# A decoder layer's prompt scores: from 64-row fp32 products to stacked full-height rounded ones

## The chip, the cores and the metric

The kernel runs on one core of a Trainium2 chip. The metric is the device time of one launch in microseconds. Before the change three runs took 1153.15, 1154.85 and 1155.16 us; the median is 1154.85. A core has five engines with a queue each: TensorE (PE, with its weight loads shown as PEld), VectorE (DVE), ScalarE (ACT), GpSimd (POOL) and SyncE (SP), which here issues the loads.

## The reference

One layer of a hybrid decoder, for a prompt of 512 tokens with 16 meta tokens ahead of it and for 8 samples of 8 new tokens, each with 2048 cached ones. The width is 1024.

```python
h = rmsnorm(x) @ w_in                     # q, k, v; GDN's q, k, v, z, b, a; two gates
# differential attention: 4 heads, two maps (m) of 64 columns each
s = einsum('bqhmd,bkhmd->bhmqk', q_blk * 64 ** -0.5, k)
s = where(k_pos <= q_pos, s, -inf)
pr = softmax(s)
o_a = einsum('bhqk,bkhe->bqhe', pr[:, :, 0] - lam * pr[:, :, 1], v)
# gated DeltaNet (GDN): causal convolution of width 4, then 4 heads in chunks of 64 tokens
mix = sigmoid(gate_a) * (o_a @ w_branch_a) + sigmoid(gate_b) * (o_b @ w_branch_b)
x = x + rmsnorm(mix @ w_out)
# ConvFFN of width 2816: up-projected gate rows, causal convolution of width 3, GELU
up, gate = split(rmsnorm(x) @ w_ffn_in)
x = x + rmsnorm((gelu(dwconv(gate)) * up) @ w_down)
```

Everything is float32, with an accuracy near that of float32 throughout.

## The kernel before

**Precision.** A float32 matrix is split into a rounded part `hi`, cast to float32r, and a rest `lo`, the difference. A product is then three rounded products: hi x hi, lo x hi and hi x lo. `split` does this for weights: ScalarE casts and VectorE subtracts (`whi`, `wlo`, lines 314 and 315). Products of plain float32 exist too; one of these leaves two records in the trace. All products are issued by the helper `mm` (line 272), all transposes at line 420, so a product is known by its tiles: `ps_d` and others with `xhi`, `xlo` are projections of the normed input, `ps_s` with `KT`, `qb` or `page`, `pT` the sampled attention over the paged cache (32 columns of the array wide), `ps_m` the prompt scores.

**Prompt attention.** For each of the four heads `da_keys` makes the keys and the values: a projection to `kvt` (128 rows: 64 of map 0 over 64 of map 1; columns are tokens), from which GpSimd copies `kT` for the scores. The scaled queries `qT` of all heads were made before, in the same layout. `prompt_rows` then takes four blocks of 128 queries. Block i has n = 16 + 128(i+1) keys: 144, 272, 400, 528. A score product multiplies 64 rows of `qT` by 64 rows of `kT`, map 0 on rows 0 to 63 and map 1 on rows 64 to 127 of the array; the two maps' results stand side by side in the one tile `ps_m`, which has one buffer. [...] VectorE's `score` moves a result to `S0` or `S1`, adds the causal mask to the last 128 keys and keeps the row maximum in `mx`; ScalarE takes the exponential, VectorE combines the maps, TensorE transposes and multiplies by the values.

**FFN.** The input projection of the FFN has 22 steps, each for 128 columns of gate and 128 of up. The activations stand as four quadrants: two halves of the 1024 rows and two halves of the tokens of 290 columns each. The first PLAIN steps multiply plainly: 8 half-depth products of 12 matmuls, 96 matmuls in all. The other steps use a scheme of seven products (`p1` to `p7`, tiles `ps_t`, `ps_g`, `ps_d`, `ps_s`) over sums of weight blocks (`sw`, split to `hw`, `lw`) and sums of activation blocks (made once, from `gf` to `fhit`, `flot`): 7 x 12 = 84 matmuls.

**What sets the order.** Each part is a Python generator. `merge` interleaves them: it advances the one whose share of work is furthest behind, counting work only on TensorE, and a `yield DELAY[k]` keeps a stream out until that many microseconds of modelled TensorE work have been issued. There are 31 delays, from the GDN chain (0 to 20), the key making (21), the prompt attention (22 to 25) and the sampled attention (26 to 30). A scheduler then fixes the order on each engine, and on the chip each engine runs its list in order, with waits on semaphores. Tiles come from pools with a fixed number of buffers; a tile's first write waits until the last reader of the buffer's former tile is done. The pool `gproj` holds, among others, `pre` (two buffers, the GDN convolution's input, from `conv_tile`), `kt` and `vt` (its results).

Of the kernel before, what the change touches and what calls it, by code (L numbers as in the profile page):

```python
# [18 lines left out]
SEQ = 512  # L19
NM = 16  # L20
# [15 lines left out]
NT = SEQ + NS + NM  # L36
CS = SEQ
CM = SEQ + NS
# [14 lines left out]
def _lay_out_constants():  # L53
# [76 lines left out]


DELAY = (
    13.61, 3.59, 0.94, 0.6, 6.0, 1.52, 1.66, 1.43, 1.32, 1.05, 0.93, 0.17, 26.0, 0.69, 0.9, 0.77,
    0.09, 0.85, 0.38, 2.28, 0.14, 0.6, 0.74, 2.36, 6.91, 0.77, 1.4, 5.18, 1.38, 1.46, 12.26,
)
KEYS = 2
CUT_S = 832
# [2 lines left out]
WRAW, WLO = 3, 4  # L140
LOADS_AHEAD = 5
NC = 290
PLAIN = 3
TAILS = 4
FINE = 8
MAIN_1 = 600.0
# [4 lines left out]
class Body:  # L151
# [1008 lines left out]
    def da_keys(self, pool, h, res):  # L1160
        nc, a, o = self.nc, self.a, self.o
        w = a["w_in"][0]
        for part, c0 in ((0, C_K), (1, C_V)):
            wt = self.weight(w, c0 + 128 * h)
            full = self.t(pool, [128, NT], "kvt", bufs=2)
            for half in HALF_T:
                out = []
                yield from self.dense_steps(wt, self.x, half, out)
                for p, c in out:
                    nc.scalar.copy(full[:, c[0] : c[1]], p)  # L1170
                yield DELAY[21] if half is HALF_T[1] else 0.0
            if part == 0:
                kT = self.t(pool, [128, NM + SEQ], "kT", bufs=KEYS)
                nc.gpsimd.tensor_copy(kT[:, NM:], full[:, 0:SEQ])
                nc.gpsimd.tensor_copy(kT[:, 0:NM], full[:, CM:NT])
                nc.gpsimd.tensor_copy(self.kTm[:, h], full[:, CM:NT])
                nc.gpsimd.tensor_copy(self.kTs[:, h, :], full[:, CS:CM])
            p1 = self.ps4("t")
            for i in range(4):
                self.transpose(p1[:, i], full[:, 128 * i : 128 * i + 128])  # L1180
            p2 = self.ps("t")
            self.transpose(p2[:NTL, :128], full[:, CS:NT])
            nat = self.t(pool, [128, 4, 128], "kno" if part == 0 else "v", bufs=2 if part == 0 else KEYS)
            if part == 0:
                tail = self.t(pool, [128, 128], "knt", bufs=2)
                op = o["new_k_prompt"][0, 0, :, h].rearrange("t m d -> t (m d)")
                os = o["new_k_sample"][0, :, :, h].rearrange("b t m d -> (b t) (m d)")
            else:
                tail = self.vt[:, 128 * h : 128 * h + 128]
                op = o["new_v_prompt"][0, 0, :, h]  # L1190
                os = o["new_v_sample"][0, :, :, h].rearrange("b t e -> (b t) e")
            nc.vector.tensor_copy(nat, p1)
            nc.vector.tensor_copy(tail[:NTL], p2[:NTL, :128])
            nc.gpsimd.dma_start(op[NM:].rearrange("(i p) e -> p i e", p=128), nat)
            nc.gpsimd.dma_start(os, tail[0:64])
            nc.gpsimd.dma_start(op[14:16], tail[64:66])
            nc.gpsimd.dma_start(op[0:14], tail[66:80])
            yield 0.0
        res.update(kT=kT, v=nat)

    def lam(self, tmp):
        nc, a, keep = self.nc, self.a, self.keep
# [77 lines left out]
    def prompt_rows(self, pool, h, st, on, order):  # L1280
        nc = self.nc
        kT, v = st["kT"], st["v"]
        e = slice(128 * h, 128 * h + 128)
        for i in order:
            n = NM + 128 * (i + 1)
            pr = [self.t(pool, [128, 528], f"S{m}", bufs=2) for m in range(2)]
            mxs = [self.t(self.keep, [128, 2], "mx", bufs=4) for m in range(2)]
            cuts = ((0, n),) if n <= 512 else ((0, n - 128), (n - 128, n))
            for lo, hi in cuts:
                p = self.t(self.psum_m, [128, 2, 512], "ps_m", bufs=1)[:, :, : hi - lo]  # L1290
                for m in range(2):
                    r = slice(64 * m, 64 * m + 64)
                    self.mm(p[:, m], self.qT[r, h, 128 * i : 128 * i + 128], kT[r, lo:hi], start=True, stop=True)
                for m in range(2):
                    s, mx = pr[m], mxs[m]
                    w = n - 128 - lo
                    if lo < n - 128:
                        self.score(s[:, lo : n - 128], p[:, m, :w], self.zeros(w), -3e38, mx[:, 0:1])
                    if hi == n:
                        self.score(s[:, n - 128 : n], p[:, m, w:], self.c("causal"), mx[:, 0:1], mx[:, 1:2])  # L1300
            rs = []
            for s, mx in zip(pr, mxs):
                nm = self.t(self.keep, [128, 1], "nm", bufs=4)
                nc.vector.tensor_scalar(nm, mx[:, 1:2], -1.0, None, op0=ALU.mult)
                sm = self.t(self.keep, [128, 1], "sm", bufs=4)
                nc.scalar.activation(s[:, :n], s[:, :n], AF.Exp, bias=nm, accum_out=sm)
                rc = self.t(self.keep, [128, 1], "rc", bufs=4)
                nc.vector.reciprocal(rc, sm)
                if s is pr[1]:
                    nc.vector.tensor_tensor(out=rc, in0=rc, in1=self.nlam, op=ALU.mult)  # L1310
                rs.append(rc)
            yield DELAY[24]
            nc.vector.tensor_scalar(pr[1][:, :n], pr[1][:, :n], rs[1], None, op0=ALU.mult)
            at = pr[0]
            nc.vector.scalar_tensor_tensor(
                out=at[:, :n], in0=at[:, :n], scalar=rs[0], in1=pr[1][:, :n], op0=ALU.mult, op1=ALU.add
            )
            aT = self.t(pool, [128, 5, 128], "aT", bufs=2)
            tp = self.ps4("t")
            for j in range(i + 1):  # L1320
                self.transpose(tp[:, j], at[:, NM + 128 * j : NM + 128 * j + 128])
            nc.scalar.copy(aT[:, : i + 1], tp[:, : i + 1])
            tq = self.ps("t")
            self.transpose(tq[:NM, :128], at[:, 0:NM])
# [445 lines left out]
    def ffn_in(self, firsts, sf, gx):  # L1770
# [203 lines left out]

        sts, waiting = [{"m": m} for m in range(PLAIN)], []
        st = sts[0]
# [23 lines left out]
        for st in sts[2:]:  # L2000
# [5 lines left out]
            plain_end(st)  # L2006
        nxt = loads(PLAIN)
        weights_g(nxt)
# [200 lines left out]
```

## Time and profile before

| what | value |
| --- | --- |
| runs | 1153.15, 1154.85, 1155.16 us |
| the profiled execution's own time | 1153.75 us |
| its span, first to last instruction | 1152.0 us |
| mean granted TensorE clock | 0.996 |
| instructions | 23616 |
| memory read / written | 146.12 / 9.88 MB |

The profiled execution is a single run; its span leaves out 1.75 us around the first and the last instruction. Busy times count the records of an engine and don't say that it ran at its best. A row of a view names the source line, the engine, the operation, output and input tiles without their numbers, shape and type. What stands in brackets or behind the bar is the engine's idle time just before, and what ended it. A float32r product is shown with type f32.

### The profile page before, as it was taken

To read this page: it belongs to the slowest core of one execution; us is meant where nothing else is said; L and a number is where in the kernel's file an instruction comes from. 1 tells how busy PE (TensorE), PEld (TensorE's weight loads), DVE (VectorE), ACT (ScalarE), POOL (GpSimd) and SP (SyncE) were. 2 spreads that over 40 slices of the span, in tenths; PEclk is the share of its full clock that TensorE was granted. 3 is DMA by queue.
4 is the path that set the end of the run, shared out by engine and by line. 5 is a ranking of instruction groups with operands and counts; after the bars stand their busy time and mean duration, and the time that the engine had idled before them with its cause. 6 is when DMAs were issued, how large, how long until landed. Compare 5 with 4: busy or idle time off the path is not lost.

```text
span 1152.0 us, 23616 instructions
## 1 busy us (share of the span) xinstructions
PE 1115.3 (97%) x8683; PEld 1004.1 (87%) x8683; DVE 717.3 (62%) x1875; ACT 539.0 (47%) x1308; POOL 220.5 (19%) x342
## 2 busy tenths in 40 slices
PE   6999999999999999999999999999999999999997
PEld 5887887787787787789999977899999999999996
DVE  5456666695486377474343765499889889832323
ACT  5334445464464365352332344365565656732321
POOL 2022221020120010010000003333455444200000
PEclk9999999999999999999999999999999999999999
DMA  7366335737756956823232364323333332432322
GB/s 208 81 223 188 102 104 195 255 110 251 237 159 216 290 173 209 263 74 80 55 90 69 110 187 153 95 70 102 102 87 100 93 94 73 144 97 74 102 75 83
DMA packets 184347, 157.56 MB, mean 137 GB/s; under 512 B 12570, under 2 KB 146273, under 8 KB 184231
## 3 DMA queue, kind: packets, MB, share of 16 engines
q1 hardware_dynamic: 179713, 147.53, 42.0%
q0 software_dynamic: 3264, 5.16, 1.5%
q10 hardware_dynamic: 1254, 3.35, 1.0%
q8 instruction: 69, 1.13, 0.4%
q14 instruction: 47, 0.39, 0.1%
HBM read 146.12 MB, written 9.88 MB: 135 GB/s over the span
## 4 chain that ended last, share of the span: by engine, by line
PE 73%; issue 13%; DVE 6%; ACT 3%; POOL 3%; DMA 1%; SPq 0%; DVEq 0%; POOLq 0%; ACTq 0%
PE ps_d L272 26%; PE ps_t L272 18%; PE ps_g L272 15%; PE ps_s L272 7%; PE ps_t L420 7%; ACT KT L1399 1%; PE ps_m L272 1%; DVE cy L650 1%; DMA lk<-in_da_lambda_k 1%; POOL grr L384 1%; POOL gf L384 0%; DVE wlo L315 0%; DMA page<-in_cache_v 0%; POOL hss L384 0%; DVE row L970 0%
## 5 line engine op out<-in xcount | busy, mean ns | idle before, releaser
L272 PE MATMUL ps_d<-xhi,whi 128*128 128x256 f32 (+2 forms) x704 | 217.8, 310 | 0.2 <-DVE qm L1128 0.2
L315 DVE TENSOR_TENSOR wlo<-wraw,whi 128x512 fp32r<-128x512 f32 x196 | 137.9, 720 | 122.4 <-ACT whi L314 121.6
L272 PE MATMUL ps_d<-xhi,wlo 128*128 128x256 f32 (+2 forms) x704 | 213.3, 303 | 0.7 <-DVE wlo L315 0.7
L272 PE MATMUL ps_d<-xlo,whi 128*128 128x256 f32 (+2 forms) x704 | 212.8, 303 | 0.3 <-DVE xlo L315 0.2
L314 ACT CAST whi<-wraw 128x512 fp32r<-128x512 f32 (+1 forms) x198 | 117.3, 612 | 179.1 <-PE ps_d L272 93.8
L272 PEld LDWEIGHTS ps_d<-xhi,whi 128*128 128x128 f32 x704 | 133.6, 190 | 5.8 <-issue 4.2
L272 PEld LDWEIGHTS ps_d<-xlo,whi 128*128 128x128 f32 x704 | 133.9, 190 | 3.3 <-issue 2.4
L272 PEld LDWEIGHTS ps_d<-xhi,wlo 128*128 128x128 f32 x704 | 133.6, 190 | 2.5 <-issue 1.0
L1399 ACT COPY KT<-ps_t 128x512 f32<-128x512 f32 x106 | 57.2, 603 | 31.3 <-PE ps_t L420 30.8
L420 PE MATMUL ps_t<-consts,page 128*128 128x128 f32 x512 | 67.8, 279 | 0.3
L272 PE MATMUL ps_t<-fhit,hw 128*128 128x290 f32 x228 | 68.0, 298 | 0.0
L272 PE MATMUL ps_t<-flot,hw 128*128 128x290 f32 x228 | 67.7, 297 | 0.0
L272 PE MATMUL ps_t<-fhit,lw 128*128 128x290 f32 x228 | 67.6, 297 | 0.0
L420 PEld LDWEIGHTS ps_t<-consts,page 128*128 128x128 f32 x512 | 55.6, 140 | 13.8 <-issue 6.7
L314 ACT CAST hw<-sw 128x512 fp32r<-128x512 f32 x76 | 47.2, 622 | 41.4 <-PE ps_g L272 19.9
L315 DVE TENSOR_TENSOR lw<-sw,hw 128x512 fp32r<-128x512 f32 x76 | 60.1, 790 | 6.7 <-ACT hw L314 6.6
L272 PEld LDWEIGHTS ps_t<-flot,hw 128*128 128x128 f32 x228 | 43.2, 190 | 0.0
L272 PEld LDWEIGHTS ps_t<-fhit,lw 128*128 128x128 f32 x228 | 43.1, 189 | 0.0
L272 PEld LDWEIGHTS ps_t<-fhit,hw 128*128 128x128 f32 x228 | 43.0, 189 | 0.0
L1887 DVE SCALAR_TENSOR_TENSOR fy<-fpre,fw,fy 128x592 f32<-128x592 f32 x44 | 36.5, 830 | 2.5 <-ACT fy L1885 1.8
L272 PE MATMUL ps_s<-page,pT 128*32 128x256 f32 x512 | 35.3, 385 | 1.8 <-DMA page<-in_cache_v 1.6
L272 PE MATMUL ps_s<-KT,qb 128*32 128x256 f32 x512 | 35.7, 385 | 0.6
(688 smaller groups left out, 2990.1 us busy)
## 6 DMA issues: line engine op xcount, KB each, us to landing
page<-in_cache_k SPq DMA_DIRECT2D x128, 256.0 KB, 4.2
page<-in_cache_v SPq DMA_DIRECT2D x128, 256.0 KB, 4.4
wraw<-in_w_in SPq DMA_DIRECT2D x88, 256.0 KB, 3.0
wraw<-in_w_ffn_in SPq DMA_DIRECT2D x50, 256.0 KB, 3.0
wraw<-in_w_down SPq DMA_DIRECT2D x40, 256.0 KB, 3.2
raw<-in_w_ffn_in SPq DMA_DIRECT2D x38, 256.0 KB, 2.9
wraw<-in_w_out SPq DMA_DIRECT2D x16, 256.0 KB, 2.9
x<-in_x_prompt SPq DMA_DIRECT2D x4, 512.0 KB, 8.7
```

Of the source, the lines that this page charges most:

```text
L272: return self.nc.tensor.matmul(out, lhsT, rhs, **kw).ins
L314: self.nc.scalar.copy(hi, raw)
L315: (eng or self.nc.vector).tensor_tensor(out=lo, in0=raw, in1=hi.bitcast(F32), op=ALU.subtract)
L384: nc.gpsimd.tensor_tensor(out=dst, in0=dst, in1=self.mhalf[:rows, :n], op=ALU.pow)
L420: self.nc.tensor.transpose(out, in_, self.ident[:k, :k])
L650: nc.vector.scalar_tensor_tensor(out=y, in0=pre[:, j : j + n], scalar=self.cw[:, ch, 24 + j : 25 + j], in1=y, op0=ALU.mult, op1=ALU.add)
L1399: copy(kt[:, :, 128 * j : 128 * j + 128], tp)
L1887: nc.vector.scalar_tensor_tensor(out=y, in0=pre[:, j : j + 592], scalar=fw[:, m, 16 + j : 17 + j], in1=y, op0=ALU.mult, op1=ALU.add)
```

## The change

Three edits. First, the scores become products of full height (128 rows) in float32r. `stacked_keys` makes two key tiles a head, one for each map: the rounded keys in the map's own 64 rows, and the rest (key less rounded key) in the other 64. The tile of map 0 is `kT`, cast by ScalarE; that of map 1 takes the buffer of the GDN's `kt` (heads 0, 2) or `vt` (heads 1, 3) and is cast by GpSimd. VectorE makes the rests. `stacked_queries` makes, for each block, a `pre` tile with two 128-row query matrices a map: the rounded query in both halves, and the query's rest in both halves. The first product gives rounded q x (rounded k + rest of k), the second, accumulated on it, rest of q x both. Block 3 is now cut in 272 and 256, so its second cut has 128 keys without a mask too, and one more `score` operation a map; `mx` gets a third column for its maximum. Second, PLAIN goes from 3 to 2: the FFN's third step is done by seven products. Third, 13 of the 31 delays have new values.

```diff
 DELAY = (
-    13.61, 3.59, 0.94, 0.6, 6.0, 1.52, 1.66, 1.43, 1.32, 1.05, 0.93, 0.17, 26.0, 0.69, 0.9, 0.77,
-    0.09, 0.85, 0.38, 2.28, 0.14, 0.6, 0.74, 2.36, 6.91, 0.77, 1.4, 5.18, 1.38, 1.46, 12.26,
+    13.61, 3.24, 1.52, 0.6, 6.2, 2.64, 2.2, 1.43, 1.32, 0.75, 0.93, 0.17, 26.0, 0.69, 1.23, 0.52,
+    0.09, 0.85, 0.93, 2.28, 0.1, 0.72, 0.74, 2.36, 6.91, 0.95, 1.4, 5.18, 1.38, 0.39, 12.26,
 )
...
-PLAIN = 3
+PLAIN = 2
...
-                kT = self.t(pool, [128, NM + SEQ], "kT", bufs=KEYS)
-                nc.gpsimd.tensor_copy(kT[:, NM:], full[:, 0:SEQ])
-                nc.gpsimd.tensor_copy(kT[:, 0:NM], full[:, CM:NT])
+                kT = self.stacked_keys(pool, h, full)
...
+    def stacked_keys(self, pool, h, full):
+
+        nc = self.nc
+        k0 = self.t(pool, [128, NM + SEQ], "kT", F32R, bufs=KEYS)
+        k1 = self.t(self.gproj, [128, NM + SEQ], ("kt", "vt")[h % 2], F32R)
+        for dst, src in ((slice(NM, NM + SEQ), slice(0, SEQ)), (slice(0, NM), slice(CM, NT))):
+            for m, k in enumerate((k0, k1)):
+                r, other = slice(64 * m, 64 * m + 64), slice(64 - 64 * m, 128 - 64 * m)
+                (nc.gpsimd.tensor_copy if m else nc.scalar.copy)(k[r, dst], full[r, src])
+                nc.vector.tensor_tensor(out=k[other, dst], in0=full[r, src], in1=k[r, dst].bitcast(F32), op=ALU.subtract)
+        return k0, k1
+
+    def stacked_queries(self, h, i):
+
+        nc = self.nc
+        qs = self.t(self.gproj, [128, 2, 2, 128], "pre", F32R, bufs=2)
+        for m in range(2):
+            r, other = slice(64 * m, 64 * m + 64), slice(64 - 64 * m, 128 - 64 * m)
+            src = self.qT[r, h, 128 * i : 128 * i + 128]
+            for d in (r, other):
+                (nc.gpsimd.tensor_copy if m else nc.scalar.copy)(qs[d, m, 0], src)
+            for d in (r, other):
+                nc.vector.tensor_tensor(out=qs[d, m, 1], in0=src, in1=qs[r, m, 0].bitcast(F32), op=ALU.subtract)
+        return qs
...
+            qs = self.stacked_queries(h, i)
             pr = [self.t(pool, [128, 528], f"S{m}", bufs=2) for m in range(2)]
-            mxs = [self.t(self.keep, [128, 2], "mx", bufs=4) for m in range(2)]
-            cuts = ((0, n),) if n <= 512 else ((0, n - 128), (n - 128, n))
+            mxs = [self.t(self.keep, [128, 3], "mx", bufs=4) for m in range(2)]
+            cuts = ((0, n),) if n <= 512 else ((0, n - 256), (n - 256, n))
             for lo, hi in cuts:
                 p = self.t(self.psum_m, [128, 2, 512], "ps_m", bufs=1)[:, :, : hi - lo]
                 for m in range(2):
-                    r = slice(64 * m, 64 * m + 64)
-                    self.mm(p[:, m], self.qT[r, h, 128 * i : 128 * i + 128], kT[r, lo:hi], start=True, stop=True)
+                    for j in range(2):
+                        self.mm(p[:, m], qs[:, m, j], kT[m][:, lo:hi], start=j == 0, stop=j == 1)
```

How the order moves, at three places. TensorE at head 0, block 3, where the first score groups stand between sampled-attention products (`ps_s`) and projections (`ps_d`); `kT_806` and `kt_807` are the two key tiles, `pre_1003` the query tile. Before:

```order
L272 MATMUL ps_m_1000<-kT_806,qT_301 128x400 x2
L272 MATMUL ps_s_721<-KT_909,qb_304 32x256 x4
L272 MATMUL ps_s_721<-KT_893,qb_304 32x256 x4
L272 MATMUL ps_d_1055<-xhi_8_87,whi_961 128x336
L272 MATMUL ps_d_1055<-xlo_9_88,whi_961 128x336
L272 MATMUL ps_m_1005<-kT_806,qT_301 128x128 x2
L272 MATMUL ps_d_1055<-xhi_8_87,wlo_962 128x336
```

After:

```order
L272 MATMUL ps_m_1016<-kT_806,pre_1003 128x272 x2
L272 MATMUL ps_m_1016<-kt_807,pre_1003 128x272 x2
L272 MATMUL ps_s_721<-KT_916,qb_304 32x256 x4
L272 MATMUL ps_s_721<-KT_900,qb_304 32x256 x4
L272 MATMUL ps_d_1088<-xhi_8_87,whi_968 128x336
L272 MATMUL ps_m_1023<-kT_806,pre_1003 128x256 x2
L272 MATMUL ps_m_1023<-kt_807,pre_1003 128x256 x2
L272 MATMUL ps_d_1088<-xlo_9_88,whi_968 128x336
```

A group of two products became one of four, in about the same place; the second group stands one projection product earlier.

VectorE at head 3, between the scores of block 3 and those of block 2 (`pre_2490`, `cy_2501` before and `pre_2540`, `cy_2551` after belong to the GDN convolution; line 1230 is line 1253 after). Before:

```order
L1230 ISA S_526_2571,mx_2573<-ps_m_2579,consts_66,mx_2573 128x128
L1230 ISA mx_2573 128x1
L1304 TENSOR_SCALAR nm_2584<-mx_2572 128x1
L1304 TENSOR_SCALAR nm_2590<-mx_2573 128x1
L657 SCALAR_TENSOR_TENSOR q_2262<-pre_2490,cy_2501 128x512
L657 SCALAR_TENSOR_TENSOR q_2262<-pre_2490,cy_2501 128x16
L657 SCALAR_TENSOR_TENSOR q_2262<-pre_2490,cy_2501 128x64
L1308 RECIPROCAL rc_2588<-sm_2586 128x1
L1308 RECIPROCAL rc_2594<-sm_2592 128x1
L1230 ISA S_541_2643,mx_2645<-ps_m_2647,consts_66 128x272
```

After:

```order
L1221 TENSOR_TENSOR pre_2628<-qT_301,pre_2628 64x128
L1253 ISA S_520_2596,mx_2598<-ps_m_2606,consts_66,mx_2598 128x128
L1253 ISA mx_2598 128x1
L1221 TENSOR_TENSOR pre_2628<-qT_301,pre_2628 64x128
L1327 TENSOR_SCALAR nm_2621<-mx_2598 128x1
L1221 TENSOR_TENSOR pre_2628<-qT_301,pre_2628 64x128 x2
L640 COPY tailT_2701<-ps_t_2699 27x128
L315 TENSOR_TENSOR wlo_2799<-wraw_2793,whi_2795 128x512
L657 SCALAR_TENSOR_TENSOR kt_2456<-pre_2540,cy_2551 128x512
L657 SCALAR_TENSOR_TENSOR kt_2456<-pre_2540,cy_2551 128x16
L657 SCALAR_TENSOR_TENSOR kt_2456<-pre_2540,cy_2551 128x64
L1331 RECIPROCAL rc_2619<-sm_2617 128x1
```

Four subtractions for the query tile `pre_2628` now stand among the last score operations of the group before, and a weight split with the convolution's last steps behind them.

VectorE in the FFN, where the first step of seven products is prepared (`wlo` and `lw` are rests of weights, `flot` of activation sums, `sw` sums of weight blocks, `fy` and `gt` end a plain step). Before:

```order
L315 TENSOR_TENSOR wlo_10145<-wraw_10140,whi_10144 128x512
L315 TENSOR_TENSOR wlo_10148<-wraw_10142,whi_10144 128x512
L315 TENSOR_TENSOR wlo_10219<-wraw_10214,whi_10218 128x512
L315 TENSOR_TENSOR flot_1908_10315<-gf_1863_10052,fhit_1907_10314 128x580
L1887 SCALAR_TENSOR_TENSOR fy_10094<-fpre_9914,fw_9625,fy_10094 128x592
L315 TENSOR_TENSOR flot_1908_10315<-gf_1864_10055,fhit_1907_10314 128x580
L1887 SCALAR_TENSOR_TENSOR fy_10094<-fpre_9914,fw_9625,fy_10094 128x592
L315 TENSOR_TENSOR wlo_10222<-wraw_10216,whi_10218 128x512
L1805 TENSOR_TENSOR sw_10296<-sw_10294,wraw_10283 128x512
```

After:

```order
L315 TENSOR_TENSOR wlo_10369<-wraw_10364,whi_10368 128x512
L315 TENSOR_TENSOR wlo_10372<-wraw_10366,whi_10368 128x512
L315 TENSOR_TENSOR lw_10380<-sw_10375,hw_10379 128x512
L1828 TENSOR_TENSOR sw_10383<-wraw_10366,sw_10377 128x512
L1910 SCALAR_TENSOR_TENSOR fy_10314<-fpre_10134,fw_9845,fy_10314 128x592
L315 TENSOR_TENSOR lw_10388<-sw_10377,hw_10387 128x512
L1910 SCALAR_TENSOR_TENSOR fy_10314<-fpre_10134,fw_9845,fy_10314 128x592
L315 TENSOR_TENSOR lw_10392<-sw_10383,hw_10391 128x512
L315 TENSOR_TENSOR flot_1912_10396<-gf_1883_10272,fhit_1911_10395 128x580
```

The splits of two plain weights for the third step are gone, and the sums and splits of the first seven-product step stand in their place, ahead of the activation sums' splits.

More of the change, by code (lines that the diff above doesn't have):

```diff
@@ L1291, in prompt_rows @@
                 for m in range(2):
-                    r = slice(64 * m, 64 * m + 64)
-                    self.mm(p[:, m], self.qT[r, h, 128 * i : 128 * i + 128], kT[r, lo:hi], start=True, stop=True)
+                    for j in range(2):
+                        self.mm(p[:, m], qs[:, m, j], kT[m][:, lo:hi], start=j == 0, stop=j == 1)
                 for m in range(2):
                     s, mx = pr[m], mxs[m]
-                    w = n - 128 - lo
-                    if lo < n - 128:
-                        self.score(s[:, lo : n - 128], p[:, m, :w], self.zeros(w), -3e38, mx[:, 0:1])
+                    w, j = min(n - 128, hi) - lo, 2 if lo else 0
+                    self.score(s[:, lo : lo + w], p[:, m, :w], self.zeros(w), mx[:, 0:1] if lo else -3e38, mx[:, j : j + 1])
                     if hi == n:
-                        self.score(s[:, n - 128 : n], p[:, m, w:], self.c("causal"), mx[:, 0:1], mx[:, 1:2])
+                        self.score(s[:, n - 128 : n], p[:, m, w:], self.c("causal"), mx[:, j : j + 1], mx[:, 1:2])
             rs = []
```

## The prediction

> **What bounds the kernel now.** I read the page first: the span, the busy times, the chain that ended last.
>
> ```profile
> span 1152.0 us, 23616 instructions
> PE 1115.3 (97%) x8683; PEld 1004.1 (87%) x8683; DVE 717.3 (62%) x1875; ACT 539.0 (47%) x1308; POOL 220.5 (19%) x342
> PE 73%; issue 13%; DVE 6%; ACT 3%; POOL 3%; DMA 1%; SPq 0%; DVEq 0%; POOLq 0%; ACTq 0%
> ```
>
> TensorE is busy for 97% of the span and carries most of the chain. A product taken off it is worth its own time, and work added to another engine costs nothing until a product waits for it. Two stretches matter, so I cut the span by stage: prompt attention lies in 55 to 215 us, the GDN chain in 215 to 510, the first FFN steps in 750 to 785. The columns are the stretch, its length, busy time of PE, PEld, DVE, ACT and POOL, granted clock, DMA share, GB/s.
>
> ```profile
> 55.00:215.00 160.00, 156.71 (x1293) 129.73 (x1291) 100.65 (x385) 75.59 (x204) 37.10 (x77) 1.00 0.53 166
> 215.00:510.00 295.00, 288.14 (x2587) 228.63 (x2587) 188.87 (x635) 151.37 (x429) 39.75 (x64) 1.00 0.64 204
> 750.00:785.00 35.00, 34.77 (x248) 34.62 (x247) 33.32 (x57) 19.87 (x40) 11.49 (x11) 0.95 0.27 77
> ```
>
> In the first, PE is idle for 3.3 us of 160 and VectorE free for 59. In the third both are full: VectorE works 33.3 of 35 us. Next the score tile's own instructions, and who waited for them:
>
> ```profile
> L272 PEld LDWEIGHTS ps_m<-kT,qT x80: 182/184/186, 78.6 to 211.5; 64*128 64x128 f32 x80
> L272 PE MATMUL ps_m<-kT,qT x80: 272/441/600, 78.7 to 211.6; 64*128 64x400 f32 x32, 64*128 64x128 f32 x16, 64*128 64x272 f32 x16, 64*128 64x144 f32 x16
>   DVE S L1230: 13.0, 10
> ```
>
> Each score product is two records of 64 rows; a head has five groups (144, 272, 400, and 400 with 128 columns) of four records, 20 groups in all. VectorE waits for the products, not they for it.
>
> **Scores on TensorE.** A group's price is what it adds between ordinary products:
>
> ```profile
> 80.78 0.32 PE L272 MATMUL ps_d<-xlo,whi 128*128 128x336 f32 x1
> 81.03 0.49 PE L272 MATMUL ps_m<-kT,qT 64*128 64x128 f32 x4
> 81.46 0.42 PE L272 MATMUL ps_d<-xhi,wlo 128*128 128x336 f32 x1
> 81.72 0.31 PE L272 MATMUL ps_d<-xhi,whi 128*128 128x336 f32 x1
> ...
> 82.95 0.32 PE L272 MATMUL ps_d<-xhi,wlo 128*128 128x336 f32 x1
> 83.19 0.94 PE L272 MATMUL ps_m<-kT,qT 64*128 64x400 f32 x4
> 84.07 0.42 PE L272 MATMUL ps_d<-xhi,whi 128*128 128x336 f32 x1
> 84.33 0.32 PE L272 MATMUL ps_d<-xlo,whi 128*128 128x336 f32 x1
> 84.48 0.32 PE L272 MATMUL ps_d<-xhi,wlo 128*128 128x336 f32 x1
> ```
>
> Ordinary products of 336 columns start 0.154 us apart, 0.46 ns a column. From 82.95 to 84.33 stand two of them and the 400-column group: 1.38 - 0.31 = 1.07 us. From 80.78 to 81.72: 0.94 - 0.31 = 0.63 us for 128 columns. A line through both gives 0.66 for 144 and 0.86 for 272. A head costs 0.66 + 0.86 + 1.07 + (1.07 + 0.63) = 4.29 us, four heads 17.2. About 0.4 us of each group doesn't depend on its columns: the pause around products of another array shape.
>
> After, a group is four full-height rounded products of the shape of their neighbours, so without the pause. At 0.46 ns a column a head takes 4 x (144 + 272 + 400 + 272 + 256) = 5376 columns, 2.47 us, and all heads 9.9. No rounded product of this trace is narrower than 256 columns; the 144-column ones have no row of their own. Their bounds are the rounded rate and the rate of narrow unrounded full-height products, which this piece of the chain shows (18 records of 128 columns, two a product):
>
> ```profile
> 93.87 2.01 PE ps_t L272 x18
> ```
>
> That is 0.223 us a product, 1.74 ns a column. So four of 144 take 0.27 to 1.0 us, and the gain is 17.2 - 9.9 = 7.3 or 17.2 - 12.8 = 4.4 us. I take 4.4: the rows for narrow full-height products all show the slow rate. [...]
>
> Page products of 32 columns are another shape. The new order breaks their runs into 75 instead of 71:
>
> ```profile
> PEld ps_s L272 <- issue: 2.0, 7, 0.6
> ```
>
> At 2.0/7 = 0.29 us a pause, four more cost 1.1 us (bounds 0 and 4 x 0.6 = 2.4).
>
> **Work moved to the other engines.** Rows for the price:
>
> ```profile
> L861 DVE TENSOR_TENSOR lm<-gv,consts 64x512 f32<-64x512 f32 x8 | 5.2, 679 | 4.1 <-ACT gv L844 4.1
> L2124 DVE TENSOR_TENSOR yn<-ps_t,lnfp 64x128 f32<-64x128 f32 x8 | 2.2, 273 | 0.0
> L839 ACT COPY qS<-ps_g 64x128 f32<-64x128 f32 x4 | 1.0, 262 | 0.1
> L1230 DVE CUSTOM_DVE_ANT_0 S<-ps_m,consts,mx 128x128 f32<-128x128 f32 x32 | 10.8, 345 | 0.3
> L1177 POOL COPY kTs<-kvt 128x64 f32<-128x64 f32 x4 | 0.9, 233 | 0.0
> L1174 POOL COPY kT<-kvt x4: 627/791/862, 61.6 to 155.4; 128x512 f32<-128x512 f32 x4
> ```
>
> VectorE gets 64 query subtractions of 64x128 (0.273: 17.5 us), eight key subtractions of 64x512 (0.679: 5.4) with eight of 16 columns (under 0.2 each: 1.5), and eight more score operations (under 0.345: 2.0 with their read-outs): some 26 us on 100.65 of 160, so 79%. ScalarE gets 32 casts at 0.262 and the key copies, about 12 us on 75.6; GpSimd 32 casts, about 0.23 each, less the old key copies' bulk, on 37.1. None of these is the bound by its sum; TensorE's queue covers them while it has projection products in front of the score. If that cover is gone, the block's chain is exposed: cast 0.26, two subtractions of each map 0.55, hand-over 0.3, about 1.1 us, and every product queued behind the score waits with it. [...]
>
> One place is tight: head 3. Its query tiles use the two "pre" buffers that the GDN convolution also takes, so the tile of the 400-column group waits for the 272+256 group to be read; between these stand on TensorE only eight products of 256 and sixteen of 336 columns (8 x 0.118 + 16 x 0.154 = 3.4 us), while VectorE has its convolution operations, the last score operations (four at 0.345) and the four subtractions (1.1). On ScalarE the casts stand behind an exponential over the sampled scores:
>
> ```profile
> L1479 ACT ACTIVATE S<-S,nm 128x2112 f32<-128x2112 f32 x4 | 8.2, 2062 | 3.8 <-DVE nm L1477 3.8
> ```
>
> 2.06 + 0.52 (two casts) + 1.1 + 0.3 = 4.0 us, and some of VectorE's other work, against 3.4: I take 1.5 us of waiting in all, with bounds of 0 and 16 blocks x 1.1 = 17.6, nearest the low end because PE's waits in this stretch are 3.3 us now.
>
> **Third FFN step.** Seven half-depth products instead of eight:
>
> ```profile
> 755.09 6.45 PE ps_t L272 x48
> ...
> 777.68 4.83 PE ps_t L272 x36
> ...
> 758.16 0.76 DVE L315 TENSOR_TENSOR flot<-fhit,fhit 128x580 fp32r<-128x580 f32 x1
> 760.53 0.84 DVE L1887 SCALAR_TENSOR_TENSOR fy<-fpre,fw,fy 128x592 f32<-128x592 f32 x1 [1.61 <-ACT fy L1885]
> ```
>
> 48 products take 6.45 us, 0.134 each; 12 fewer save 1.6. VectorE must have the sums' splits and the weight splits ready one step sooner, in the stretch where it is nearly full. Walking its new order with these durations, I find the last split ready 0.2 us late at the first product of the fourth step, and earlier everywhere else: the gain is kept, and the loss has as its upper bound a wait like this one at the FFN's start:
>
> ```profile
> 747.11 0.60 PE L420 MATMUL ps_t<-consts,y 128*128 128x128 f32 x4
> 749.62 0.40 PE L272 MATMUL ps_s<-fhi,hw 128*128 128x290 f32 x1 [1.92 <-ACT hw L314]
> 749.86 0.29 PE L272 MATMUL ps_s<-flo,hw 128*128 128x290 f32 x1
> ...
> 751.03 0.45 PE L272 MATMUL ps_s<-flo,hw 128*128 128x290 f32 x1
> 751.28 0.44 PE L272 MATMUL ps_s<-fhi,lw 128*128 128x290 f32 x1
> 751.52 0.44 PE L272 MATMUL ps_s<-fhi,hw 128*128 128x290 f32 x1
> ```
>
> The wait costs 2.2 us, and afterwards products start 0.245 apart instead of 0.134 for a while (clock 0.95 in that stretch); with 14 such products the price is 2.2 + 1.5 = 3.7. No DMA is added in either part: a plain step and a seven-product step both load four quarters of a megabyte, and their places in SP's queue stay; the small stores in POOL's queue are not on the chain.
>
> **Delays.** Eleven of the 13 reach an instruction; they shift a piece by one or two rows among PE's products. At most they give back PE's idle time in the two long stretches, 3.3 + 6.9 = 10.2 us; they could lose as much. No row gives a sign: zero, with 3 us either way in the range, a third of that idle time.
>
> **The sum.** -4.4 - 1.6 + 1.1 + 1.5 = -3.4 us. The profiled execution took 1153.75 (span 1152.0), so 1150.35; the median of the three runs, 1154.85, is 1.1 above it, so 1151.4 for a median.
>
> **Rivals.**
> - Slower by the other engines' queues. Without waits the sum is -4.9; each waiting block adds 1.1, so from seven of sixteen blocks on the kernel is slower by over 2.3. With eight: +3.9, 1158.8. For it: VectorE at 79% of the stretch, ACT's casts behind exponentials, the shared buffers. Against it: 59 us free, and in the new order several us of projection products between most casts and their scores.
> [...]
> - Larger gain: narrow rounded products at the full rate and no waits: -7.3 - 1.6 + 1.1 = -7.8, 1147.0.
> - The seven-product step starves: -3.4 + 1.6 (gain gone) + 3.7 = +1.9, and with one more waiting block +3.0, 1157.9. VectorE's 33.3 of 35 us speaks for it.
>
> **How the numbers follow.** 0.2% of the time, 2.3 us, is about what a measurement here can tell from no change. Forecast (1148.5 to 1152.5) 0.46; larger gain 0.12; no change 0.14; queues 0.21; starving step 0.07. Faster 0.58, same 0.14, slower 0.28. The range reaches from the larger gain with 2.5 us of the delays, 1144.5, to the queue case with one, 1160; the forecast's own range is 1148.5 to 1153.
>
> **What would show it.** Right: the score groups' products with no issue pause beside them and starts 0.46 ns a column apart; 144-column ones at 0.25 us; VectorE near 127 us in 55 to 215; PE's idle time there below 6 us with its longest wait at head 3; three chain pieces of 36 or 24 products where the third step's 48s stood. Wrong: waits of PE for the query tiles in most heads, a wait or a lower clock at 770 to 800 us, or a GDN stretch that is longer by several us.

## The result and the profile after

The changed kernel takes 1163.0 us (median of six runs, 1160.1 to 1171.0) against 1154.0 us before: a ratio of 1.0088, 95% interval 1.0062 to 1.0113. Ratios and intervals, here and below, compare all the runs of the two kernels and aren't quotients of the two medians. It is 9 us slower, where 3.4 us faster was forecast, and it lies above the range. The profiled execution after took 1160.12 us, at the fast end of its runs; its page begins:

```profile
span 1158.4 us, 23774 instructions
PE 1113.8 (96%) x8671; PEld 1006.7 (87%) x8671; DVE 756.7 (65%) x1977; ACT 544.6 (47%) x1352; POOL 239.8 (21%) x378
PE 67%; DVE 12%; issue 12%; ACT 3%; POOL 3%; DMA 2%; SPq 0%; DVEq 0%; POOLq 0%; ACTq 0%
```

TensorE's busy time hardly moved, VectorE's grew by 39 us, and its share of the chain doubled from 6 to 12%. By stage (the columns as before: PE, PEld, DVE, ACT, POOL, clock, DMA share, GB/s):

```profile
55.00:215.00 160.00, 152.92 (x1259) 134.07 (x1257) 122.96 (x474) 84.28 (x238) 49.88 (x109) 0.99 0.49 149
215.00:510.00 295.00, 285.41 (x2560) 222.73 (x2560) 179.51 (x608) 145.15 (x401) 36.58 (x63) 0.99 0.67 214
...
765.00:825.00 60.00, 57.62 (x421) 56.55 (x421) 58.79 (x99) 33.65 (x64) 30.26 (x35) 1.00 0.29 85
```

TensorE is idle for 7.1 us of the prompt stretch (3.3 before), 9.6 of the GDN stretch (6.9) and 2.4 of 765 to 825 us, where it was never idle before. The score tile's view, with the 144-column group between projections:

```profile
L272 PE MATMUL ps_m<-kT,pre x40: 228/342/428, 79.4 to 205.3; 128*128 128x272 f32 x16, 128*128 128x256 f32 x8, 128*128 128x400 f32 x8, 128*128 128x144 f32 x8
...
  PE ps_m L272: 7.3, 4
  issue: 1.1, 3
  DVE pre L1221: 0.3, 1
...
  DVE S L1253: 7.3, 4
```

```profile
164.85 0.27 PE L272 MATMUL ps_d<-xhi,whi 128*128 128x256 f32 x1
164.96 0.34 PE L272 MATMUL ps_m<-kT,pre 128*128 128x144 f32 x2
165.13 0.39 PE L272 MATMUL ps_m<-kt,pre 128*128 128x144 f32 x2
165.36 0.32 PE L272 MATMUL ps_d<-xlo,whi 128*128 128x256 f32 x1
165.52 0.29 PE L272 MATMUL ps_d<-xhi,wlo 128*128 128x256 f32 x1
```

The products came out better than forecast: four of 144 columns take 0.40 us in this group and 0.47 to 0.49 in the other three, not 1.0. The least disturbed groups of 272, 256 and 400 columns take 0.58, 0.47 and 0.73, so a head costs 0.40 + 0.58 + 0.73 + 0.58 + 0.47 = 2.76 us and all four 11.0, against 17.2 before: 6.2 us less where nothing else holds a group up. And a query tile kept a weight load waiting once, for 0.3 us (the line with DVE pre). So the loss isn't in the score products themselves. The experiments look for it.

One measure is used throughout. For a kernel I sum the ordinary distances of TensorE's products other than scores (0.118 us for 256 columns, 0.154 for 336, 0.110 for a transpose, 0.060 for one of 32 array columns), and compare when two kernels reach the same sum, half-clock time taken off. The three places are where before stands at 226 us (prompt scores done), 500 (GDN done) and 751 (FFN begun). A plus is later than before, in us, from the one profiled execution of each. It is good to about 1 us: PLAIN 2 alone and PLAIN 4, whose products are those of before up to 751 us, stand 0.5 to 0.8 us ahead at 226 and 0.6 to 1.2 at 500.

| kernel | at 226 | at 500 | at 751 |
| --- | --- | --- | --- |
| the changed kernel | -0.1 | +3.5 | +3.2 |
| scores alone | -0.2 | +5.9 | +5.3 |
| VectorE's load alone | +3.9 | +3.6 | +4.2 |
| order alone | +2.5 | +10.2 | +10.3 |
| delays alone | -1.1 | +5.1 | +6.6 |
| scores, counted as before | -2.5 | +2.9 | +2.4 |
| scores for heads 0 to 2, counted as before | -2.3 | -2.6 | -2.5 |

### The profile page after: what moved, and what is told of

The parts are those of the page before. It is cut to its first block, busy times and chain, and to the rows that moved or that the text cites. A ratio compares the mean times of both kernels' runs of the same rounds, so it can differ in the third digit from the quotient of the medians.

```text
span 1158.4 us, 23774 instructions
## 1 busy us (share of the span) xinstructions
PE 1113.8 (96%) x8671; PEld 1006.7 (87%) x8671; DVE 756.7 (65%) x1977; ACT 544.6 (47%) x1352; POOL 239.8 (21%) x378
## 4 chain that ended last, share of the span: by engine, by line
PE 67%; DVE 12%; issue 12%; ACT 3%; POOL 3%; DMA 2%; SPq 0%; DVEq 0%; POOLq 0%; ACTq 0%
PE ps_d L272 23%; PE ps_t L272 16%; PE ps_g L272 15%; PE ps_s L272 6%; PE ps_t L420 6%; DVE wlo L315 1%; DVE S L1253 1%; DVE cy L650 1%; DMA wraw<-in_w_in 1%; POOL grr L384 1%; PE ps_m L272 1%; DMA page<-in_cache_k 1%; DVE lw L315 1%; POOL hss L384 1%; DVE row L970 0%
## 5 line engine op out<-in xcount | busy, mean ns | idle before, releaser
L315 DVE TENSOR_TENSOR wlo<-wraw,whi 128x512 fp32r<-128x512 f32 (+1 forms) x194 | 143.2, 753 | 110.9 <-ACT whi L314 110.0
L314 ACT CAST whi<-wraw 128x512 fp32r<-128x512 f32 x196 | 115.8, 612 | 160.9 <-PE ps_d L272 81.2
L315 DVE TENSOR_TENSOR lw<-sw,hw 128x512 fp32r<-128x512 f32 x80 | 75.5, 943 | 5.3 <-ACT hw L314 5.2
L272 PE MATMUL ps_t<-fhit,hw 128*128 128x290 f32 x240 | 72.1, 300 | 1.6 <-ACT p L1857 1.1
L272 PE MATMUL ps_t<-flot,hw 128*128 128x290 f32 x240 | 71.2, 297 | 0.0
L272 PE MATMUL ps_t<-fhit,lw 128*128 128x290 f32 x240 | 71.2, 297 | 0.0
L1908 ACT ACTIVATE fy<-fpre,fw 128x592 f32<-128x592 f32 x22 | 19.4, 884 | 50.0 <-DVE fpre L1868 49.9
L908 POOL DMA_DIRECT2D out_new_gdn_sample<-st x4 | 3.8, 946 | 168.5 <-ACT gv L892 79.7
```

The source lines that it names most:

```text
L272: return self.nc.tensor.matmul(out, lhsT, rhs, **kw).ins
L314: self.nc.scalar.copy(hi, raw)
L315: (eng or self.nc.vector).tensor_tensor(out=lo, in0=raw, in1=hi.bitcast(F32), op=ALU.subtract)
L908: nc.gpsimd.dma_start(o["new_gdn_sample"][0, :, h].rearrange("b k v -> k b v"), state)
L1908: nc.scalar.activation(y, pre[:, 0:592], AF.Identity, bias=fw[:, m, 19:20], scale=fw[:, m, 16:17])
```

## The experiments

**The three parts, each alone.** The first takes the changed kernel with the old delays and PLAIN 3:

```diff
-    13.61, 3.24, 1.52, 0.6, 6.2, 2.64, 2.2, 1.43, 1.32, 0.75, 0.93, 0.17, 26.0, 0.69, 1.23, 0.52,
-    0.09, 0.85, 0.93, 2.28, 0.1, 0.72, 0.74, 2.36, 6.91, 0.95, 1.4, 5.18, 1.38, 0.39, 12.26,
+    13.61, 3.59, 0.94, 0.6, 6.0, 1.52, 1.66, 1.43, 1.32, 1.05, 0.93, 0.17, 26.0, 0.69, 0.9, 0.77,
+    0.09, 0.85, 0.38, 2.28, 0.14, 0.6, 0.74, 2.36, 6.91, 0.77, 1.4, 5.18, 1.38, 1.46, 12.26,
...
-PLAIN = 2
+PLAIN = 3
```

> The kernel before with the stacked rounded scores alone (old delays, PLAIN 3). Theory V (VectorE's extra work delays the copies on which TensorE's transposes wait, so the scores eat their own gain): 0 to 5 us slower than before, with VectorE near 123 us in the prompt stretch and TensorE's waits there up by 4 us or more. Theory D (the new delays are the loss, the scores a gain as predicted): 2 to 6 us faster.

Measured: 1161.3 us, ratio 1.0062 (1.0045 to 1.0080), 6.3 us slower. The scores lose by themselves, by a little more than theory V's 0 to 5 us; theory D falls.

The kernel before with PLAIN alone (PLAIN = 3 to 2):

> The kernel before with PLAIN 2 alone. Theory F (the third step starves on VectorE's splits): 0 to 3 us slower than before, with TensorE waiting for VectorE or ScalarE between 765 and 810 us. As predicted (12 products fewer at no wait): 1.6 us faster.

Measured: 1157.0 us, 1.0025 (1.0013 to 1.0036), 2.0 us slower, as theory F had it.

The kernel before with the new delays alone:

> The kernel before with the 13 new delays alone. Theory V: within 2 us of before. Theory D: 4 to 9 us slower. What I had put into the sum: 0, with 3 either way.

Measured: 1178.6 us, 1.0217 (1.0192 to 1.0243), 23.6 us slower, far past both theories and anything I had allowed for.

The changed kernel with PLAIN back at 3:

> The changed kernel with PLAIN back at 3, so scores and delays together. If the parts add: the sum of the two single effects. If the delays were fitted to the new scores: less than the scores alone by 2 us or more. Against the changed kernel (9 us slower than before) it shows the third step's share: 1.6 us more if the step gains as predicted, 0 to 3 less by theory F.

Measured: 1160.7 us, 1.0049 (1.0030 to 1.0069), 5.7 us slower. The parts don't add: 6.3 + 23.6 would be 29.9. On the new scores the new delays cost nothing (5.7 against 6.3 with the old ones), though the 2 us that fitted delays should gain aren't there either; on the old scores they are ruinous. What a set of delays is worth depends on the work that it orders. The changed kernel has 9.0, so 3.3 are left for the third step, though these two come from different sessions.

Why the delays alone cost so much is seen in the GDN stretch of that kernel (three windows, then TensorE's longest wait between 440 and 510 us, then the whole run's clock):

```profile
460.00:472.00 12.00, 9.04 (x102) 5.98 (x99) 6.63 (x30) 3.26 (x6) 0.35 (x2) 1.00 0.84 269
472.00:506.00 34.00, 26.65 (x156) 19.65 (x156) 6.08 (x16) 7.24 (x21) 0.58 (x1) 0.50 0.30 99
506.00:520.00 14.00, 14.00 (x95) 11.92 (x95) 6.74 (x16) 4.92 (x16) 0.96 (x1) 1.00 0.15 37
```

```profile
PE ps_s L272 <- DMA page<-in_cache_v: 6.7, 5, 1.7
```

```profile
core 0: 1177.5 us, clock 0.980
```

TensorE waits 6.7 us for pages of cached values, 1.7 of them just ahead of a stretch of 34 us at half clock and the rest at its start and inside it. The stretch takes 17 us of full clock away. All five runs of this kernel show a clock of 0.978 to 0.982, where before shows 0.992 to 0.998; 1177.5 x 0.020 = 24 us of full clock are missing, against 1152 x 0.004 = 5 before. The late pages and the low clock stand together; which brought the other isn't shown.

**Load or order?** VectorE's subtractions are added to the kernel before, into a tile that nothing reads:

```diff
...
+            for m in range(2):
+                r, other = slice(64 * m, 64 * m + 64), slice(64 - 64 * m, 128 - 64 * m)
+                src = self.qT[r, h, 128 * i : 128 * i + 128]
+                for d in (r, other):
+                    dummy = self.t(pool, [128, 128], "dummy", bufs=1)
+                    nc.vector.tensor_tensor(out=dummy[d], in0=src, in1=src, op=ALU.subtract)
```

> The kernel before with 64 subtractions of 64x128 for the queries and 32 of 64x128 and eight of 64x16 for the keys added on VectorE, into a tile that nothing reads; TensorE's order and products as before. Theory L (VectorE's load alone makes the waits): 4 to 12 us slower than before, since it has the load of the scores without their gain. Theory O (the order of TensorE's work is what changed, because the order's rule counts a rounded column at a quarter of an unrounded one): within 2 us of before.

Measured: 1158.0 us, 1.0027 (1.0016 to 1.0039), 3.2 us slower, a little under theory L's range and over theory O's. TensorE's order is exactly that of before. The table shows it all in the prompt stretch (+3.9), and nothing more behind it.

The scores alone without the query subtractions:

```diff
-            for d in (r, other):
-                nc.vector.tensor_tensor(out=qs[d, m, 1], in0=src, in1=qs[r, m, 0].bitcast(F32), op=ALU.subtract)
...
-                        self.mm(p[:, m], qs[:, m, j], kT[m][:, lo:hi], start=j == 0, stop=j == 1)
+                        self.mm(p[:, m], qs[:, m, 0], kT[m][:, lo:hi], start=j == 0, stop=j == 1)
```

> The scores alone (old delays, PLAIN 3) with the 64 query subtractions left out; the second product of each map takes the rounded query again, so the rests of the queries are not in the scores. TensorE's products keep their number and shape. Theory L: 4 us or more faster than the scores alone (which were 6 us slower than before), so about before or faster. Theory O: within 2 us of the scores alone.

Measured: 1161.6 us, 1.0049 (1.0035 to 1.0063). Less load, and still 6.8 us slower, as theory O had it: the query subtractions aren't the main loss. By the table's measure this kernel is 2.6 us ahead at 226 and 3.3 behind at 500, so they do cost TensorE some 2 us in the prompt stretch, and the loss lies behind it.

The scores alone, counted as before by the rule that interleaves the streams:

```diff
                         self.mm(p[:, m], qs[:, m, j], kT[m][:, lo:hi], start=j == 0, stop=j == 1)
+                        self.work += 0.42e-3 * (hi - lo)
```

> The scores alone, with the work that the order's rule counts for a score product doubled, so that a group counts as much as before and the streams interleave nearly as before. Theory O: 4 us or more faster than the scores alone. Theory L: within 2 us of the scores alone.

Measured: 1162.5 us, 1.0063 (1.0049 to 1.0076). Theory O falls: with the count put right the kernel is no faster, so the count alone isn't what the stacked scores lose by. The table says more: with this order TensorE is 2.5 us ahead at 226 us, as load and products would give, and then loses 5.4 in the GDN stretch. In the order itself the products there still stand some places away from before. The query tiles of head 3 share buffers with the GDN convolution, and the scheduler may be going around that; no run shows it alone.

So the order was moved with nothing else:

```diff
                     self.mm(p[:, m], self.qT[r, h, 128 * i : 128 * i + 128], kT[r, lo:hi], start=True, stop=True)
+                    self.work -= 0.84e-3 * (hi - lo)
```

> The kernel before with each score product counted at half its work by the rule that interleaves the streams, as the rounded products are counted; no instruction is added or changed, only the order. Theory O2 (the GDN stretch is sensitive to any shift of the order, and that is where the stacked scores lose their gain): 3 to 8 us slower than before, the loss lying between 220 and 510 us. Theory L (load on VectorE and the other engines): within 2 us of before.

Measured: 1166.1 us, 1.0094 (1.0076 to 1.0111): 11.1 us slower with the same instructions, more than theory O2's 3 to 8; theory L falls. Of it 2.5 us are lost ahead of 226 us and 7.7 in the GDN stretch. This is the largest single effect of the study that isn't the clock:

```profile
215.00:510.00 295.00, 284.27 (x2544) 220.75 (x2537) 185.22 (x618) 146.71 (x411) 37.57 (x64) 1.00 0.66 212
```

```profile
core 0: 1162.4 us, clock 0.996
```

The clock is that of before, and TensorE's busy time in the GDN stretch is down from 288.1 to 284.3 us. Counting in the traces between 55 and 560 us: before changes 96 times from full-array products to tiled ones and back, this kernel 106 times; such a pair costs about 0.56 us from start to start where the two products would take 0.19, so ten more cost 3.7 us. Where full-array products start over 0.4 us apart, what this adds to an ordinary distance grows from 12.4 to 16.7 us. Together that is 8.0 of the 9.9 us that this kernel loses there (0.5 ahead at 78 us, 9.4 behind at 562). Scores alone has nearly this kernel's order: its other products stand 1 to 8 places away on average, in each stretch of the list. So an estimate for it is 10.2 for the order, less 6.2 for the products, with up to 3.9 for VectorE's load: 4.0 to 7.9 us behind at 500, where the table has 5.9.

**With the order kept.** Heads 0 to 2 by stacked products, head 3 as before, counted as before:

```diff
-                kT = self.stacked_keys(pool, h, full)
+                if h in STACKED:
+                    kT = self.stacked_keys(pool, h, full)
+                else:
+                    kT = self.t(pool, [128, NM + SEQ], "kT", bufs=KEYS)
...
-            qs = self.stacked_queries(h, i)
+            qs = self.stacked_queries(h, i) if h in STACKED else None
```

TensorE's order in the GDN stretch is then that of before, place by place. With scores left out, and the n-th product of the same tiles and shape compared, the 1200th to 1600th products (177 to 223 us) stand 53 places off on average in the changed kernel and in the order-alone kernel, and 3 with all four heads counted as before; in the products behind these it is 5 on average there, and over 100 for a few.

> Old delays, PLAIN 3; the scores of heads 0 to 2 by stacked rounded products, head 3 as before, and the stacked products counted by the order's rule as much as the old ones. TensorE's order in the GDN stretch is the one of before. Theory O2 (the loss is the order): 1 to 4 us faster than before, since three heads' products save 4.9 us and their load costs about 2.9. Theory W (the stacked scores lose by their own load and waits, whatever the order): 2 to 6 us slower.

> The same for heads 0 and 1 alone. Theory O2: 0.5 to 2.5 us faster than before, two thirds of the three-head effect. Theory W: 1 to 4 us slower.

> Heads 0 to 2 stacked with the query subtractions on GpSimd, order as before. If VectorE's load takes part of the gain: 1 to 2 us faster than three heads with VectorE. If GpSimd's slower operations come late: as fast or slower.

Measured on one chip, against 1154.4 us: three heads 1153.8 us, 0.9995 (0.9982 to 1.0009); two heads 1153.7 us, 0.9996 (0.9985 to 1.0007); three heads with the query subtractions on GpSimd 1151.4 us, 0.9981 (0.9969 to 0.9994). Theory W falls for these heads: with the order kept, they lose nothing. Theory O2's gain is seen in the table (2.3 us at 226, still 2.5 at 751), but the medians of the first two move by only 0.7 us, inside their intervals; their runs' clocks spread from 0.992 to 0.998, which is 7 us; so the forecast gain isn't shown by the times. The third kernel is 3.0 us faster than before by the medians and 2.2 by the ratio, and beats both kernels. VectorE's load in the prompt stretch is lower there:

```profile
55.00:215.00 160.00, 154.88 (x1315) 133.81 (x1314) 119.25 (x453) 83.58 (x229) 46.26 (x101) 1.00 0.55 171
```

```profile
55.00:215.00 160.00, 155.11 (x1309) 134.53 (x1307) 110.79 (x412) 83.36 (x230) 67.04 (x141) 0.99 0.54 169
L1227 POOL TENSOR_TENSOR pre<-qT,pre 64x128 fp32r<-64x128 f32 x48 | 25.1, 523 | 2.9
```

The first line is three heads with VectorE, the other two with GpSimd: an operation takes 0.523 us there instead of 0.287, and VectorE has 8.5 us less to do. In single profiled executions both are 2.6 us ahead at 500 us, so where the further 2.4 us of the medians come from isn't shown.

What is left is head 3. All four heads counted as before lost 7.6 us (on another chip, against its own runs of before) where three heads lost nothing, and stacking head 3 is all that differs. TensorE's waits for GDN's normalised keys (`kn`) from 215 to 510 us (us in all, times, longest), all four heads first, then three:

```profile
PE ps_t L420 <- DVE kn L792: 3.9, 2, 2.2
```

```profile
PE ps_t L421 <- DVE kn L793: 1.2, 1, 1.2
```

The second is that of before too. In all TensorE is idle for 11.3 us of that stretch with four heads and for 7.0 with three. Whether head 3's cost comes from the few products that moved, from its load, or from GDN waiting for the buffers that head 3 takes, no run separates; four heads with buffers of their own would test the last.

The move of the query subtractions to GpSimd once more, in the changed kernel's order (PLAIN 3):

```diff
-                nc.vector.tensor_tensor(out=qs[d, m, 1], in0=src, in1=qs[r, m, 0].bitcast(F32), op=ALU.subtract)
+                nc.gpsimd.tensor_tensor(out=qs[d, m, 1], in0=src, in1=qs[r, m, 0].bitcast(F32), op=ALU.subtract)
```

> Scores and new delays (PLAIN 3) with the 64 query subtractions on GpSimd instead of VectorE. Theory L: 2 to 5 us faster than scores and delays together (which were 5.7 us slower than before). [...]

Measured: 1161.1 us, 1.0041 (1.0022 to 1.0060), against 1.0049 (1.0030 to 1.0069) without it: no difference that these runs can tell, though one of some 2 us isn't ruled out. Theory L's 2 to 5 us aren't seen.

**The third FFN step.** In PLAIN 2 alone, around the first seven-product step (GpSimd, then ScalarE, then TensorE):

```profile
768.83 3.16 POOL L1805 TENSOR_TENSOR sw<-wraw,raw 128x512 f32<-128x512 f32 x1
771.95 1.29 POOL L1805 TENSOR_TENSOR sw<-raw,raw 128x512 f32<-128x512 f32 x1
```

```profile
772.02 0.62 ACT L314 CAST hw<-sw 128x512 fp32r<-128x512 f32 x1 [3.90 <-POOL sw L1805]
...
774.39 0.38 ACT L1834 COPY p<-ps_t 128x290 f32<-128x290 f32 x1
```

```profile
774.82 0.40 PE L272 MATMUL ps_t<-fhit,hw 128*128 128x290 f32 x1 [1.91 <-ACT p L1834]
```

GpSimd's first sum takes 3.16 us where the next takes 1.29; ScalarE's cast waits for it. The copy of a finished product, which TensorE needs, stands behind this cast and three more operations: 1.91 us. Three attempts on the cause follow. First, the two sums of that step on VectorE:

```diff
-            combine(st, "s1", a21, a22, ALU.add)
+            eng = nc.vector if st["m"] == PLAIN else nc.gpsimd
+            combine(st, "s1", a21, a22, ALU.add, eng)
...
-            combine(st, "s3", a11, a21, ALU.subtract)
+            combine(st, "s3", a11, a21, ALU.subtract, eng)
```

> PLAIN 2 alone, with the two GpSimd weight sums of the first seven-product step (s1, s3) made by VectorE instead. Theory G (GpSimd's sum, 3.2 us instead of 1.3, held ScalarE's queue and with it the copy that TensorE waited for, 1.9 us): 1.5 to 3.5 us faster than PLAIN 2 alone, so about 0 to 1 us faster than before. Theory F (VectorE itself is full): no faster than PLAIN 2 alone, or slower by up to 1.4 us for the two operations.

Then the order of the loads in SP's queue:

```diff
             st, raw = {"m": m}, []
+            st["raw"] = self.raw_w(w, DFF + 128 * m)
...
-            st["raw"] = self.raw_w(w, DFF + 128 * m)
```

> PLAIN 2 alone, with the two loads of the left weight blocks issued ahead of the two of the right ones in every seven-product step. Theory Q (in SP's queue a load of the right blocks waits for its buffer and holds the left blocks' loads behind it, so that ScalarE's casts come late in the first steps): 2 to 4 us faster than PLAIN 2 alone. Theory F (VectorE and GpSimd are simply full in the first steps): within 1 us of it.

And one plain step more than before (PLAIN = 4):

> The kernel before with four plain steps instead of three, so 12 products more. If the switch to seven products costs nothing at step four: 1.6 us slower. If the first seven-product steps also lose time to their preparation before the change: 0 to 3 us faster, since the preparation gets another plain step of time.

Measured in this order: sums on VectorE 1157.1 us, 1.0030 (1.0018 to 1.0042); other loads 1157.9 us, 1.0020 (1.0008 to 1.0033); PLAIN 4 1157.4 us, 1.0017 (1.0005 to 1.0030). The first two are no faster than PLAIN 2 alone; the third fits 1.6 us for 12 products more. The stretch from 765 to 825 us of before, PLAIN 2, PLAIN 2 with VectorE's sums, PLAIN 2 with the other loads, and PLAIN 4:

```profile
765.00:825.00 60.00, 60.00 (x448) 59.98 (x447) 55.35 (x98) 35.48 (x68) 28.72 (x35) 1.00 0.36 102
```

```profile
765.00:825.00 60.00, 56.16 (x408) 54.99 (x407) 55.09 (x95) 32.68 (x64) 32.63 (x35) 1.00 0.31 89
```

```profile
765.00:825.00 60.00, 55.60 (x407) 54.67 (x406) 56.02 (x96) 33.00 (x64) 30.94 (x33) 1.00 0.31 89
```

```profile
765.00:825.00 60.00, 56.14 (x409) 54.94 (x408) 55.40 (x98) 32.00 (x62) 33.06 (x33) 1.00 0.31 88
```

```profile
765.00:825.00 60.00, 60.00 (x448) 59.99 (x447) 49.41 (x87) 32.26 (x66) 23.42 (x29) 1.00 0.32 93
```

With three plain steps or four TensorE is never idle; with two it is idle for 3.8 to 4.4 us in all three kernels. Theories G and Q fall as single causes: with VectorE's sums the 1.91 us at 774 are gone, and waits of 2.4, 1.4 and 0.6 us between 807 and 824 take their place; with the other loads the 1.91 us stay. The reading that fits all five is that the third plain step is the time in which VectorE, GpSimd and ScalarE prepare the first seven-product step. 1.6 us of products are saved and 3.8 of idle time bought: 2.2 us slower, where 2.0 were measured. The fourth plain step only costs its 12 products.

## Why the prediction was wrong

- **Delays, taken at zero with 3 us either way: the step that failed, in what it left out.** The delays do cost nothing on the new scores; that is luck, for the 2400th to 3600th products stand 29 places away from those of scores alone. But I took the order of TensorE's work to be moved by the delays alone, "by one or two rows", and found the score groups in about the same place. Neither holds: the delays alone move the 2400th to 3600th products by 64 places on average and cost 23.6 us, past the 10.2 that I took as the most they could lose. And the rule that interleaves the streams counts a score group by type: 3.36e-3 us a column before, 1.68e-3 after, so 18.1 us of modelled work became 9.0, and much behind the scores stands elsewhere. For that the sum had no term. The order alone cost 11.1 us on the old scores; in the changed kernel 3.6 us are lost between 226 and 500 us. That the order is what costs there follows from the like orders, the estimate above and the three heads that lost nothing; putting the count right for all four heads didn't bring the time back, so a part of the cause, at head 3, stays open. No rival named the order: the queue rival came nearest in time (1158.8), but by waits for query tiles, and a product of a score waited only 0.3 us for one.
- **Scores, -4.4 taken from 4.4 to 7.3:** -6.2. The mechanism was right, the choice for the narrow products wrong. The pause at a change of shape, 0.4 us a group before, is gone beside the undisturbed new groups of 256 and 400 columns: they take 0.47 and 0.73 us, and four products at 0.46 ns a column make 0.47 and 0.74.
- **Switches, +1.1:** about right. Runs of products of 32 array columns rose from 79 to 82 between 55 and 560 us, where four more were forecast. All changes of shape together fell from 96 pairs to 82, because the old score groups were changes too; their pauses are in the scores' term.
- **Waits, 1.5 at head 3:** not as waits for query tiles. Head 3 was rightly called tight, but what came late with it, with the count put right, was GDN's work behind the scores, and it cost more than 1.5. The 0.3 us of hand-over in the forecast was my estimate, and no run shows it: the one weight load that waited for a query tile started 0.05 us behind the subtraction's end (187.57 to 187.62 us). What the load costs is spread: 3.9 us with VectorE's part alone. VectorE's 122.96 us were forecast as 127. The cover I named, projection products ahead of a score, does hide the query tiles. It doesn't hide what stands behind their subtractions in VectorE's queue, as this piece of the changed kernel's chain shows (start, length, what; KT copies transposed cached keys, and the next transposes wait for it):

```profile
102.15 1.32 PE ps_t L420 x12
103.47 0.69 DVE KT L1422
...
104.20 0.29 DVE pre L1221
...
104.52 0.16 DVE rc L1331
...
104.72 0.30 DVE pre L1221
...
105.03 0.16 DVE rc L1333
105.19 0.61 DVE KT L1422
...
105.85 0.31 PE ps_t L420
```

- **FFN, -1.6:** +2.0 alone; in the changed kernel's profile 2.4 us of idle time were bought with the 1.6 saved. I walked VectorE's list with its durations, and left out that GpSimd makes two of the sums, one of which took 3.16 us, and that ScalarE's one queue carries casts and copies. The rival gave it 0.07 and 3.7 us of waiting, near the 3.8 of idle time in PLAIN 2 alone; that it also struck out the 1.6 saved was too much, and the chance was too low.
- **The sum.** The changed kernel stands level at 226 us, is 3.2 us behind at 751, loses 0.8 in the FFN's first steps and 2.4 to the clock (1158.4 x 0.006 = 7.0 us against 4.6): that makes the 6.4 us by which its profiled span is longer. The remaining 2.6 us of the medians go with the clock: runs at 0.994 to 0.995 take 1160.1 to 1161.3 us, those at 0.987 and 0.988 take 1170.5 and 1171.0.

## What to carry to other kernels

Where a rule or a table of numbers orders the work, ask first what the change does to the rule's inputs: here a cheaper product type was counted as less work, and on the old products the order so moved cost 11.1 us, more than the 6.2 that the new ones save. Compare orders far behind the edit, and test the order alone, with the same instructions. Before taking away a step that looks like pure cost, list what every other engine does during it, not only the busiest.

## What the runs showed of the hardware

TensorE's granted clock was 0.50 for some stretches, in other places from kernel to kernel: 750.4 to 753.7 us before, 472 to 506 us with the delays alone. In the changed kernel's profile there are two ahead of the end:

```profile
76.40:79.70 3.30, 3.30 (x18) 3.30 (x17) 0.00 (x0) 0.01 (x1) 0.00 (x0) 0.50 1.05 379
482.60:485.90 3.30, 3.30 (x22) 1.72 (x21) 0.76 (x3) 0.46 (x2) 0.00 (x0) 0.50 0.68 192
```

With the tenths of a microsecond at their edges (clock 0.72 and 0.71, 0.66 and 0.78) they last 3.4 us, and each takes 1.7 us of full clock away. Just ahead TensorE counts as busy for 3.39 and 2.34 of 3.40 us:

```profile
72.90:76.30 3.40, 3.39 (x31) 3.19 (x31) 1.50 (x6) 1.90 (x4) 2.54 (x5) 1.00 1.03 358
479.10:482.50 3.40, 2.34 (x15) 1.61 (x14) 1.88 (x7) 0.76 (x3) 0.00 (x0) 1.00 0.96 329
```

What starts or ends such a stretch isn't shown. In the 34 us of the delays-alone kernel TensorE was busy for 6.23 of the first 10 us, 7.88 of the next 10 and 12.53 of the last 14.

GpSimd's sums of two 128x512 weight blocks varied: in PLAIN 2 alone one took 3.16 us, with VectorE busy for its first 2.0, and the next 1.29, with VectorE idle. In the changed kernel's profile, with VectorE busy nearly all the while beside each (1.70 of 1.74 us at the least), 33 of the 40 took 1.28 to 1.31 us and seven 1.67 to 2.22, so whether VectorE is busy doesn't by itself tell a long one from a short one.
